# Dilated attention: another order of the tokens in each chunk of 128, and copies of the queries in block order

## The chip, the cores and the metric

The kernel runs on one core of a Trainium2 chip. The metric is the device time of one execution in microseconds (us); the median of three runs of the kernel before is 2824.8 us. Engines are named as the profile names them: PE (TensorE matmuls), PEld (its weight loads), DVE (VectorE), ACT (ScalarE), POOL (GpSimd), SP (SyncE, whose queue issues nearly all DMAs).

## The reference, cut to what matters

One layer over 2048 tokens of width 1024: a normalised input `h`, a large product with `w_in`, two branches and a merge. Branch a mixes the tokens of each chunk of 128 by a masked 128x128 matrix. Branch b, which the change is about, is attention with 16 heads of 64, in three patterns that differ in the stride of the keys:

```
DILATED_PATTERNS = ((128, 1), (512, 4), (2048, 16))   # (window, dilation)
def dilated_pattern(q, k, v, slopes, window, dilation):
    L = S // dilation                     # tokens t, t+dilation, ... form one sequence
    # blocks of 128 of such a sequence; each attends to itself and the block before
    s = einsum('bhrnqd,bhrnkd->bhrnqk', qb, kw) * Dh ** -0.5
    s = where(valid, s - slope * dist * dilation, -1e30)
    m = max(s);  p = exp(s - m);  l = sum(p);  o = p @ vw / l
    # back to token order
# the outputs of the three patterns are merged by l * exp(m - max m)
```

Numbers are kept to about float32 accuracy: float16 pairs (high and low part) for q, k, v and p, pairs of a reduced float32 for the large products.

## The kernel before, in words

Four parts follow each other. First the input is normalised and most columns of the product with `w_in` are made; q, k and v go to DRAM (`q_d`, `k_d`: one [128, 2048] float16 tensor a head with the high part in rows 0 to 63 and the low part below; `v_d`: one [2048, 130] a head). Then comes the attention window, then the last two products.

In the window `window` walks through 192 groups: 16 heads, in each head the patterns 2, 1, 0 (dilation 16, 4, 1), in each pattern four groups of four query blocks. A group has three stages, each a step or more after the other: `stage_s` (scores: two matmuls a block, Q against KH and KL, lines 407 and 408; DVE adds the bias and finds the row maxima, line 414; DVE writes the maxima into the output tile, line 417; ACT makes exp, line 422), `stage_t` (transposes of exp, lines 439 to 443) and `stage_o` (products with V, lines 456 to 458, and their copy by ACT, line 459). Blocks of pattern 2 have no block before, so their score matmuls have 128 columns; in pattern 1 one of four blocks is so, in pattern 0 one of sixteen; the others have 256. Between the stages stand matmuls of `fill`, the remaining products with `w_in` and `w_proj_a` (line 116), 416 us of them by the code's own count.

`cols` picks the columns of a block. Queries and keys stand in token order in SBUF, so a block of pattern 1 reads every fourth column of float16 (8 bytes apart), one of pattern 2 every sixteenth (32 bytes apart).

Loads and stores: `load_qk` loads Q, K (four DMAs) and the bias B of the next head when a head's pattern 1 begins. `load_v` loads V one pattern ahead, one DMA for each pattern: in pattern 2 each partition takes 16 neighbouring tokens (4160 bytes in a run), in pattern 1 four (1040 bytes), in pattern 0 one at a time (260 bytes). The outputs of patterns 2 and 1 (tile `ob`, two buffers) go to DRAM, `o_d`, with one DMA each, and come back in token order into OC, which has one buffer; pattern 0 writes into OC itself. `combine` then merges the three on DVE, ACT and POOL and, for a pair of heads, transposes and multiplies with the gate (`sbg`) and stores `yb`.

POOL splits the weights of `fill` into high and low parts (lines 85 and 86; `wraw` and the two parts have two buffers each), scales B and adds in `combine`. Every DMA of the window is issued by SP, in one order. PE's order is fixed by the code (`seg`). On the other engines and SP's queue a scheduler sets the order when the program is built, from its own estimates of when things are ready.

Of the kernel before, what the change touches and what calls it, by code (L numbers as in the profile page):

```python
# [16 lines left out]
P = 128  # L17
# [10 lines left out]
class Prog:  # L28
# [5 lines left out]

    # ---------------------------------------------------------------- setup
    def setup(self):
# [36 lines left out]

    # -------------------------------------------------------------- helpers
    def rsqrt_mean(self, out, ss, n):
# [12 lines left out]
    def wblock(self, wp, w, c0, width, scale=None):  # L88
        """columns c0..c0+width of a weight, as exact high and low parts;
        scale: [P, 1] that gets a scale under which no product with h leaves float16"""  # L90
        nc = self.nc
        raw = wp.tile([P, KC, width], F32, name="wraw", tag="wraw", bufs=256 // width)
        nc.sync.dma_start(out=raw, in_=w[:, c0:c0 + width].rearrange("(k p) n -> p k n", p=P))
        hi = wp.tile([P, KC, width], F32R, name="whi", tag="whi")
        lo = wp.tile([P, KC, width], F32R, name="wlo", tag="wlo")
        self.split_w(raw, hi, lo)
        if scale is not None:
            # |h @ w| <= |h| |w column| <= (32 max|g|) (32 max|w|)
            m = self.wk.tile([P, 2], F32, name="wm", tag="wm")
            nc.vector.tensor_reduce(out=m[:, 0:1], in_=raw, axis=AX.XY, op=ALU.max, apply_absolute_value=True)  # L100
            nc.vector.tensor_copy(m[:, 1:2], self.gmax)
            r = self.wk.tile([P, 2], F32, name="wr", tag="wr")
            nc.gpsimd.partition_all_reduce(r, m, P, bass_isa.ReduceOp.max)
            nc.vector.tensor_mul(m[:, 0:1], r[:, 0:1], r[:, 1:2])
            nc.vector.tensor_scalar(out=m[:, 0:1], in0=m[:, 0:1], scalar1=1.0 / 32.0, scalar2=1e-15,
                                    op0=ALU.mult, op1=ALU.max)
            nc.vector.reciprocal(out=scale, in_=m[:, 0:1])
        return hi, lo

    def mm3(self, out, st, mv, ks=range(KC), first=True, last=True, every=0):  # L110
        """out (+)= sum_k (st_hi + st_lo)[k].T @ (mv_hi + mv_lo)[k] in three products of exact parts;
        st, mv: functions of (part, k)"""
        nc = self.nc
        todo = [(a, b, k) for k in ks for a, b in ((0, 0), (0, 1), (1, 0))]
        for n, (a, b, k) in enumerate(todo):
            self.pe = nc.tensor.matmul(out, st(a, k), mv(b, k), start=first and n == 0,  # L116
                                       stop=last and n == len(todo) - 1)
            if every and (n + 1) % every == 0 and n + 1 < len(todo):
                yield every

    def seg(self, gen):
        """the next piece of gen, its PE work queued behind that of the piece before"""
        if self.last_pe is None:
            r = next(gen, None)
        else:
            with self.tc.issue_after(self.last_pe):
                r = next(gen, None)
        if self.pe is not None:
            self.last_pe = getattr(self.pe, "ins", self.pe)
        self.pe = None  # L130
        return r
# [6 lines left out]

    # ------------------------------------------------------- normalised input
    def alloc_X(self, tt):  # L140
# [70 lines left out]

    # ---------------------------------------------------------------- q and k
    def ev_qk(self, dst, s):
# [40 lines left out]

    # --------------------------------------------------------------- branch a
    def branch_a(self, hf, X):
# [64 lines left out]

    # ------------------------------------------------------------- gates of b
    def ev_bg(self, nb, qd, ps):
# [22 lines left out]

    # -------------------------------------------------------------- attention
    def load_qk(self, at, h):
# [5 lines left out]
        for j in range(2):  # L354
# [5 lines left out]
                                op0=ALU.mult, op1=ALU.add)  # L360
        return Q, KH, KL, B

    def load_v(self, at, h, p):
        nc = self.nc
        V = at.tile([P, 16, 130], F16, name="V", tag="V", bufs=4)
        vs = self.v_d[h]
        if p == 0:
            nc.sync.dma_start(out=V, in_=vs.rearrange("(n a) d -> a n d", a=P))
        elif p == 1:
            nc.sync.dma_start(out=V.rearrange("p (n q) d -> p n (q d)", q=4),  # L370
                              in_=vs.rearrange("(n a q) d -> a n (q d)", n=4, q=4))
        else:
            nc.sync.dma_start(out=V, in_=vs.rearrange("(a n) d -> a n d", a=P))
        return V

    def cols(self, t, p, b, n):
        """n = 1: columns of block b; n = 2: of block b and the next one"""
        if p == 0:
            return t[:, P * b:P * (b + n)]
        if p == 1:  # L380
            return t.rearrange("p (a q) -> p q a", q=4)[:, b // 4, P * (b % 4):P * (b % 4 + n)]
        return t.rearrange("p (a q) -> p q a", q=16)[:, b]

    def stage_s(self, at, G):
# [4 lines left out]
        pr = h // 2  # L389
        if p == 1:  # L390
            ob = G["O"].rearrange("p (n q) d -> p q n d", q=4)[:, g]
        else:
            ob = G["O"][:, 4 * g:4 * g + 4]
        G["ob"] = ob
# [25 lines left out]
        for i in range(4):  # L420
# [3 lines left out]
            for c in range(n):  # L424
                kb = 4 * g + i - (n - 1 - c)
                pairs.append((i, c, kb if p != 1 else kb % 4 * 4 + kb // 4, c == 0, c == n - 1))
        G["pairs"] = pairs
# [20 lines left out]
    def stage_o(self, at, G):  # L448
# [137 lines left out]

    # ------------------------------------------------------------- last phase
    def final(self):
# [78 lines left out]

    # -------------------------------------------------------------------- all
    def run(self):
# [53 lines left out]
def _tables():  # L723
    i = np.arange(P)
    slopes = (2.0 ** (-8.0 * np.arange(1, NH + 1, dtype=np.float32) / NH)).astype(np.float32)
    bias = np.zeros((NH, P, 640), np.float32)
    dist = i[:, None] + P - np.arange(2 * P)[None, :]
    ok = (dist >= 0) & (dist <= P)
    for p, dil in enumerate((1, 4, 16)):
        for h in range(NH):  # L730
# [4 lines left out]
    causal = (i[None, :] >= i[:, None]).astype(np.float32)  # L735
    return bias, causal

# [31 lines left out]
```

## Time and profile before

| | before |
|---|---|
| runs | 2823.9, 2824.8, 2834.3 us |
| span of the profiled execution | 2821.4 us (3.4 us under the median of the runs) |
| attention window | from 1467.7 to 2414 us |
| PE, DVE, ACT, POOL busy | 97%, 42%, 38%, 22% of the span |
| DMA engines, share of their time | 0.35 ahead of the window, 0.63 in it, 0.52 after it |

The span runs from the first to the last instruction that the profiler recorded. A busy PE can still be slow PE, since the time of a matmul is counted whatever holds it. The granted clock is 0.98 to 0.99 in all parts.

### The profile page before, as it was taken

What the parts mean: (1) busy time and instruction counts of PE and PEld (TensorE: products, weight loads), DVE (VectorE), ACT (ScalarE), POOL (GpSimd) and SP (SyncE); (2) the same over time, 40 slices, a digit from 0 to 9 for tenths busy, and PEclk for the clock granted to TensorE, in tenths of its full rate; (3) what the DMA queues carried; (4) which work ended last, traced back from release to release, by engine and by line L of the source; (5) the groups of instructions that cost most, each with busy time, mean ns of one, the idle gap of its engine ahead of it and who ended that gap; (6) DMA issues with size and microseconds to landing.
All of it is one profiled execution on the core that took longest, in us unless ns stands there. A gap on an engine that the chain in (4) does not pass through costs nothing.

```text
span 2821.4 us, 44790 instructions
## 1 busy us (share of the span) xinstructions
PE 2724.5 (97%) x17504; PEld 2273.2 (81%) x17504; DVE 1195.5 (42%) x3186; ACT 1063.8 (38%) x2039; POOL 625.6 (22%) x398
## 2 busy tenths in 40 slices
PE   6899899999999999999999999999999999899998
PEld 4779897888887889988877777777777777678887
DVE  6232104331003111013336666677677777555443
ACT  4312212122123222221126666666666666333221
POOL 2322211223233221212231221233333333100000
PEclk9999999999999999999999999999999999999999
DMA  7633402224345333202254556656677676665442
GB/s 230 177 101 85 93 16 76 67 87 134 101 136 155 93 102 84 66 28 68 67 163 115 153 149 169 166 169 182 186 213 221 192 208 187 205 208 183 153 151 74
DMA packets 489332, 381.68 MB, mean 135 GB/s; under 512 B 152224, under 2 KB 414752, under 8 KB 489120
## 3 DMA queue, kind: packets, MB, share of 16 engines
q1 hardware_dynamic: 488688, 378.75, 46.4%
q8 instruction: 137, 2.24, 0.3%
q14 instruction: 75, 0.61, 0.1%
q10 hardware_dynamic: 432, 0.07, 0.0%
HBM read 277.42 MB, written 101.32 MB: 134 GB/s over the span
## 4 chain that ended last, share of the span: by engine, by line
PE 84%; DMA 3%; DVE 3%; ACT 2%; issue 2%; POOL 1%; SPq 0%; DVEq 0%; ACTq 0%; POOLq 0%
PE pj L116 65%; PE ss L407 5%; PE ss L408 5%; PE pt L439 4%; PE po L456 1%; PE po L458 1%; PE po L457 1%; DMA wraw<-in_w_proj_b 1%; PE pt L297 1%; DMA v_d<-vst 1%; ACT junk L281 1%; DVE X L148 1%; PE pt L509 0%; POOL wlo L86 0%; DMA xl<-ya_d 0%
## 5 line engine op out<-in xcount | busy, mean ns | idle before, releaser
L116 PE MATMUL pj<-X,whi 128*128 128x512 f32 x4608 | 1472.0, 398 | 21.4 <-ACT whi L83 8.3
L116 PEld LDWEIGHTS pj<-X,whi 128*128 128x128 f32 x4608 | 868.2, 190 | 202.6 <-ACT whi L83 10.3
L116 PE MATMUL pj<-X,wlo 128*128 128x512 f32 x2304 | 915.5, 397 | 16.1 <-POOL wlo L86 10.8
L86 POOL TENSOR_TENSOR wlo<-wraw,whi 128x1024 fp32r<-128x1024 f32 (+1 forms) x176 | 458.5, 2606 | 763.7 <-ACT whi L83 688.3
L116 PEld LDWEIGHTS pj<-X,wlo 128*128 128x128 f32 x2304 | 437.9, 190 | 109.8 <-POOL wlo L86 12.7
L116 PE MATMUL pj<-whi,X 128*128 128x256 f32 x2048 | 360.7, 279 | 6.9 <-DVE vst L238 6.7
L83 ACT CAST whi<-wraw 128x1024 fp32r<-128x1024 f32 (+1 forms) x152 | 173.2, 1140 | 505.2 <-PE pj L116 445.7
L116 PEld LDWEIGHTS pj<-whi,X 128*128 128x128 f32 x2048 | 312.9, 188 | 8.2 <-issue 7.2
L414 DVE CUSTOM_DVE_ANT_0 S<-ss,B 128x256 f32<-128x256 f32 (+1 forms) x768 | 244.6, 361 | 143.7 <-PE ss L408 142.6
L116 PE MATMUL pj<-wlo,X 128*128 128x256 f32 x1024 | 285.6, 279 | 2.7 <-POOL vst L233 2.7
L422 ACT ACTIVATE S<-S,ob,iqk 128x128 f32<-128x128 f32 (+1 forms) x512 | 231.8, 525 | 95.4 <-DVE ob L417 95.3
L407 PE MATMUL ss<-KH,Q 128*128 128x256 f16 (+1 forms) x768 | 258.5, 356 | 6.9 <-DVE m L414 6.8
L408 PE MATMUL ss<-KL,Q 128*128 128x256 f16 (+1 forms) x768 | 264.7, 358 | 0.0
L443 DVE SCALAR_TENSOR_TENSOR pl<-pt,ph 128x512 f16<-128x512 f32 x320 | 203.4, 653 | 89.8 <-ACT ph L442 88.1
L442 ACT ACTIVATE ph<-pt 128x512 f16<-128x512 f32 x320 | 167.5, 560 | 119.6 <-PE pt L439 119.5
L116 PEld LDWEIGHTS pj<-wlo,X 128*128 128x128 f32 x1024 | 192.6, 188 | 2.9 <-POOL vst L233 2.9
L85 POOL TENSOR_SCALAR whi<-wraw 128x1024 fp32r<-128x1024 f32 x64 | 69.3, 1083 | 539.0 <-PE pj L116 508.6
L116 PE MATMUL pj<-WO,X 128*128 128x512 f32 x768 | 180.1, 395 | 0.9 <-ACT X L632 0.8
L116 PEld LDWEIGHTS pj<-WO,X 128*128 128x128 f32 x768 | 144.1, 188 | 36.2 <-ACT X L632 1.2
L439 PEld LDWEIGHTS pt<-ident,S 128*128 128x128 f32 x1200 | 146.1, 144 | 28.9 <-DVE pl L443 3.6
L439 PE MATMUL pt<-ident,S 128*128 128x128 f32 x1200 | 165.6, 275 | 2.7 <-DVE pl L443 2.7
L422 ACT ACTIVATE S<-S,OC,iqk 128x256 f32<-128x256 f32 (+1 forms) x256 | 131.8, 584 | 52.5 <-DVE OC L417 52.5
(105 smaller groups left out, 2422.5 us busy)
## 6 DMA issues: line engine op xcount, KB each, us to landing
wraw<-in_w_in SPq DMA_DIRECT2D x136, 512.0 KB, 4.1
V<-v_d SPq DMA_DIRECT2D x48, 520.0 KB, 4.2
o_d<-ob SPq DMA_DIRECT2D x32, 528.0 KB, 4.3
OC<-o_d SPq DMA_DIRECT2D x32, 528.0 KB, 5.2
wraw<-in_w_in SPq DMA_DIRECT2D x16, 1024.0 KB, 5.6
wraw<-in_w_proj_a SPq DMA_DIRECT2D x32, 512.0 KB, 5.3
wraw<-in_w_proj_b SPq DMA_DIRECT2D x32, 512.0 KB, 4.5
v_d<-vst SPq DMA_DIRECT2D x128, 65.0 KB, 3.5
```

The costliest lines, as they stand in the source:

```text
L83: nc.scalar.copy(hi, raw)
L85: nc.gpsimd.tensor_scalar(out=hi, in0=raw, scalar1=1.0, scalar2=0.0, op0=ALU.mult, op1=ALU.add)
L86: self.w_lo.tensor_tensor(out=lo, in0=raw, in1=hi.bitcast(F32), op=ALU.subtract)
L116: self.pe = nc.tensor.matmul(out, st(a, k), mv(b, k), start=first and n == 0, stop=last and n == len(todo) - 1)
L148: self.x_lo.tensor_tensor(out=X[k][1], in0=src, in1=X[k][0].bitcast(F32), op=ALU.subtract)
L407: nc.tensor.matmul(ps[:, i, :n], q, self.cols(KH, p, w0, n // P), start=True, stop=False)
L408: self.pe = nc.tensor.matmul(ps[:, i, :n], q, self.cols(KL, p, w0, n // P), start=False, stop=True)
L414: nc.vector.tensor_tensor_reduce(out=S[:, j, :n], in0=ps[:, i, :n], in1=B[:, bo:bo + n], scale=1.0, scalar=-3e38, op0=ALU.add, op1=ALU.max ...
L422: nc.scalar.activation(S[:, i, :rng[i]], S[:, i, :rng[i]], AF.Exp, bias=ob[:, i, 65:66], scale=self.iqk[:, pr:pr + 1])
L439: self.pe = nc.tensor.transpose(px[:, j * P:(j + 1) * P], G["S"][:, i, c * P:(c + 1) * P], self.ident)
L442: nc.scalar.activation(ph[:, :n], px[:, :n], AF.Copy, scale=PSCALE)
L443: nc.vector.scalar_tensor_tensor(out=pl[:, :n], in0=px[:, :n], scalar=PSCALE, in1=ph[:, :n], op0=ALU.mult, op1=ALU.subtract)
```

## The change

The 128 tokens of each chunk stand in another order throughout the kernel. Position i holds token `i % 8 * 16 + i // 8 % 4 * 4 + i // 32`. Tokens of one residue modulo 4 are then 32 neighbouring columns, and those of one residue modulo 16 are 8 neighbouring columns, in each chunk. The inputs x, `w_s`, `b_s`, the causal mask and the bias tables are given in that order, and the output is put back. What else changes:

- `cols` now picks keys of pattern 1 in runs of 32 columns (64 bytes) and keys of pattern 2 in runs of 8 (16 bytes).
- POOL makes two copies of Q a head in block order, `QP[2]` and `QP[1]` (a new tile with two buffers), so that a block's queries are 128 neighbouring columns.
- V of the patterns 1 and 2 and their outputs are moved by the new function `rows` with 16 DMAs each (32 or 8 partitions, pieces of 260 or 264 bytes) where one DMA did it. V has three buffers in place of four.
- The output tile of pattern 1 is written in the order of its groups.

```diff
 def load_qk(self, at, h):
 ...
-        return Q, KH, KL, B
+        QP = {0: Q}
+        for p in (2, 1):
+            QP[p] = at.tile([P, T], F16, name="QP", tag="QP")
+            n = 16 if p == 2 else 4
+            nc.gpsimd.tensor_copy(QP[p].rearrange("p (r c a) -> p r c a", r=n, c=16),
+                                  Q.rearrange("p (c r a) -> p r c a", r=n, c=16))
+        return QP, KH, KL, B
 def load_v(self, at, h, p):
-        V = at.tile([P, 16, 130], F16, name="V", tag="V", bufs=4)
+        V = at.tile([P, 16, 130], F16, name="V", tag="V", bufs=3)
 ...
-        elif p == 1:
-            nc.sync.dma_start(out=V.rearrange("p (n q) d -> p n (q d)", q=4),
-                              in_=vs.rearrange("(n a q) d -> a n (q d)", n=4, q=4))
         else:
-            nc.sync.dma_start(out=V, in_=vs.rearrange("(a n) d -> a n d", a=P))
+            for part, row in self.rows(V, vs, p):
+                nc.sync.dma_start(out=part, in_=row)
+    def rows(self, t, d, p):
+        if p == 1:
+            tv = t.rearrange("p (q n) d -> p n q d", q=4)
+            dv = d.rearrange("(n c q a) d -> n c a q d", n=4, c=4, q=4)
+            return [(tv[32 * c:32 * c + 32, n], dv[n, c]) for n in range(4) for c in range(4)]
+        dv = d.rearrange("(c r a) d -> c a r d", c=16, r=16)
+        return [(t[8 * c:8 * c + 8], dv[c]) for c in range(16)]
 def cols(self, t, p, b, n):
         if p == 1:
-            return t.rearrange("p (a q) -> p q a", q=4)[:, b // 4, P * (b % 4):P * (b % 4 + n)]
-        return t.rearrange("p (a q) -> p q a", q=16)[:, b]
+            c = b % 4 * 4
+            return t.rearrange("p (c q a) -> p q c a", c=16, q=4)[:, b // 4, c:c + 4 * n]
+        return t.rearrange("p (c r a) -> p r c a", c=16, r=16)[:, b]
 def stage_s(self, at, G):
-        if p == 1:
-            ob = G["O"].rearrange("p (n q) d -> p q n d", q=4)[:, g]
-        else:
-            ob = G["O"][:, 4 * g:4 * g + 4]
+        ob = G["O"][:, 4 * g:4 * g + 4]
 ...
-                q = self.cols(Q, p, b, 1)
+                q = Q[p][:, P * b:P * b + P]
 def stage_o(self, at, G):
-            if p == 2:
-                nc.sync.dma_start(out=od.rearrange("(a r) d -> a r d", r=16), in_=G["O"])
-            else:
-                nc.sync.dma_start(out=od.rearrange("(n a q) d -> a n (q d)", n=4, q=4),
-                                  in_=G["O"].rearrange("p (n q) d -> p n (q d)", q=4))
+            for part, row in self.rows(G["O"], od, p):
+                nc.sync.dma_start(out=row, in_=part)
```

The scheduler puts the DMAs of SP's queue in another order. Before, on SP, between the loads of V for two patterns of head 12 (`v_d_133`; `o_d_1_184` and `o_d_0_183` are the outputs of patterns 2 and 1 of head 11, a name ahead of `<-` is what is written):

```order
L373 DMA V<-v_d_133 128x2080
L179 DMA xl<-ya_d_139 128x512 x2
L342 DMA gal<-ga_d_150 128x512
L93 DMA wraw<-in_w_proj_a 128x8x128 x2
```

Now, on SP, from the output of pattern 2 of head 11 to the next weight block:

```order
L475 DMA o_d_1_184<-ob 8x16x66 x16
L377 DMA V<-v_d_133 8x16x130 x15
L345 DMA ma_d_158<-ma 128x512
L475 DMA o_d_0_183<-ob 32x4x66 x16
L479 DMA OC<-o_d_1_184 128x16x66
L342 DMA gal<-ga_d_150 128x512
L377 DMA V<-v_d_133 32x4x130 x4
L345 DMA ma_d_158<-ma 128x512
L377 DMA V<-v_d_133 32x4x130 x12
L342 DMA gal<-ga_d_150 128x512
L479 DMA OC<-o_d_0_183 128x16x66
L345 DMA ma_d_158<-ma 128x512
L93 DMA wraw<-in_w_proj_a 128x8x128
```

All 64 new DMAs of a head stand in one stretch there, the two loads of OC behind bursts, and the next weight block behind all of them.

DVE, the first pattern-2 groups of head 1 before (`m_11417` is the maxima of the first group):

```order
L414 ISA S,m_11417<-ss,B 128x128
L414 ISA m_11417 128x1
L417 TENSOR_SCALAR ob<-m_11417,niqk 128x4
L327 SCALAR_TENSOR_TENSOR tbg<-tbg,pj 128x512
L443 SCALAR_TENSOR_TENSOR pl<-pt,ph 128x512 x2
L414 ISA S,m_11494<-ss,B 128x128
```

and now (line 414 is 426, line 417 is 429; `m_11515`, `m_11592` and `m_11680` are the first three groups):

```order
L426 ISA S,m_11680<-ss,B 128x128
L426 ISA m_11680 128x1
L429 TENSOR_SCALAR ob<-m_11515,niqk 128x4
L429 TENSOR_SCALAR ob<-m_11592,niqk 128x4
L429 TENSOR_SCALAR ob<-m_11680,niqk 128x4
L327 SCALAR_TENSOR_TENSOR tbg<-tbg,pj 128x512
L426 ISA S,m_11751<-ss,B 128x128
```

The maxima of three groups are written together there, after the scores of the third; this happens in eight places of the window.

More of the change, by code (lines that the diff above doesn't have):

```diff
@@ L425, in stage_s @@
                 kb = 4 * g + i - (n - 1 - c)
-                pairs.append((i, c, kb if p != 1 else kb % 4 * 4 + kb // 4, c == 0, c == n - 1))
+                pairs.append((i, c, kb, c == 0, c == n - 1))
         G["pairs"] = pairs
@@ L724, in _tables @@
     i = np.arange(P)
+    tok = i % 8 * 16 + i // 8 % 4 * 4 + i // 32
+    inside = (tok, i // 32 * 32 + i % 8 * 4 + i // 8 % 4, i)
     slopes = (2.0 ** (-8.0 * np.arange(1, NH + 1, dtype=np.float32) / NH)).astype(np.float32)
     bias = np.zeros((NH, P, 640), np.float32)
-    dist = i[:, None] + P - np.arange(2 * P)[None, :]
-    ok = (dist >= 0) & (dist <= P)
     for p, dil in enumerate((1, 4, 16)):
+        key = np.concatenate([inside[p], P + inside[p]])
+        dist = inside[p][:, None] + P - key[None, :]
+        ok = (dist >= 0) & (dist <= P)
         for h in range(NH):
@@ L734, in _tables @@
             bias[h, :, 256 * p:256 * p + b.shape[1]] = b
-    causal = (i[None, :] >= i[:, None]).astype(np.float32)
-    return bias, causal
+    causal = (tok[None, :] >= tok[:, None]).astype(np.float32)
+    return bias, causal, tok
 def kernel(x, g_norm, w_in, w_s, b_s, g_v, w_proj_a, w_proj_b, w_out, g_final):
     arr = lambda v: np.ascontiguousarray(np.asarray(v))
-    bias, causal = _tables()
-    x2 = arr(x)[0]
+    bias, causal, tok = _tables()
+    x2 = arr(x)[0].reshape(T // P, P, D)[:, tok].reshape(T, D)
     ins = {
@@ L747 @@
         "w_in": arr(w_in)[0],
-        "wsT": arr(w_s)[0].transpose(2, 0, 1),
+        "wsT": arr(w_s)[0].transpose(2, 0, 1)[tok][:, :, tok],
         "causal": causal,
-        "bs": np.broadcast_to(arr(b_s)[0][None], (P, 8, P)),
+        "bs": np.broadcast_to(arr(b_s)[0][:, tok][None], (P, 8, P)),
         "g_v": arr(g_v)[0].reshape(KC, P).T,
@@ L767 @@
     r = run_bass_kernel_spmd(nc, [{"in_" + k: v for k, v in ins.items()}], core_ids=[0])
-    return r.results[0]["out_y"].reshape(1, T, D)
+    y = np.empty((T // P, P, D), np.float32)
+    y[:, tok] = r.results[0]["out_y"].reshape(T // P, P, D)
+    return y.reshape(1, T, D)
```

## The prediction

> **What bounds the kernel now.** I read the head of the page first, then the three stages, then one head of the attention window by its patterns.
>
> ```profile
> span 2821.4 us, 44790 instructions
> PE 2724.5 (97%) x17504; PEld 2273.2 (81%) x17504; DVE 1195.5 (42%) x3186; ACT 1063.8 (38%) x2039; POOL 625.6 (22%) x398
> PE 84%; DMA 3%; DVE 3%; ACT 2%; issue 2%; POOL 1%; SPq 0%; DVEq 0%; ACTq 0%; POOLq 0%
> core 0: us, PE busy (x) PEld busy (x) DVE busy (x) ACT busy (x) POOL busy (x), PEclk, DMA share, GB/s
> 1467.70:2414.00 946.30, 932.18 (x8028) 739.26 (x8028) 664.68 (x2395) 608.79 (x1364) 265.04 (x191) 0.99 0.63 177
> 1812.80:1833.10 20.30, 20.30 (x179) 15.98 (x176) 9.69 (x50) 11.54 (x29) 7.04 (x5) 1.00 0.73 188
> 1833.10:1851.10 18.00, 18.00 (x148) 13.34 (x145) 16.91 (x52) 11.95 (x28) 7.73 (x6) 1.00 0.36 114
> 1851.10:1873.30 22.20, 22.20 (x216) 18.95 (x213) 13.78 (x48) 14.30 (x31) 6.88 (x4) 1.00 0.67 190
> ```
>
> TensorE is the bound: 84% of the chain that ended last is PE, and in the attention window (1467.7 to 2414.0, the only stage that the change touches) it is busy 932 of 946 us. The last three rows are head 6: its pattern 2 (dilation 16), pattern 1 (dilation 4) and pattern 0 (dilation 1) steps. One head costs 946.3 / 16 = 59.1 us; this one 60.5. So a shorter score product is worth its whole length, until another queue needs as long.
>
> **The gain: score products.** Each group makes eight score matmuls. The order-of-time view of PE shows their pace by pattern; I read the distance from one start to the next, since the durations overlap.
>
> ```profile
> 1824.07 0.42 PE L407 MATMUL ss<-KH,Q 128*128 128x128 f16 x1
> 1824.31 0.42 PE L408 MATMUL ss<-KL,Q 128*128 128x128 f16 x1
> 1824.55 0.42 PE L407 MATMUL ss<-KH,Q 128*128 128x128 f16 x1
> ...
> 1841.64 0.28 PE L407 MATMUL ss<-KH,Q 128*128 128x128 f16 x1
> 1841.73 0.30 PE L408 MATMUL ss<-KL,Q 128*128 128x128 f16 x1
> 1841.85 0.41 PE L407 MATMUL ss<-KH,Q 128*128 128x256 f16 x1
> 1842.08 0.41 PE L408 MATMUL ss<-KL,Q 128*128 128x256 f16 x1
> ...
> 1501.18 0.22 PE L407 MATMUL ss<-KH,Q 128*128 128x128 f16 x1
> 1501.24 0.22 PE L408 MATMUL ss<-KL,Q 128*128 128x128 f16 x1
> 1501.30 0.27 PE L407 MATMUL ss<-KH,Q 128*128 128x256 f16 x1
> 1501.41 0.27 PE L408 MATMUL ss<-KL,Q 128*128 128x256 f16 x1
> ```
>
> Pattern 2, keys 32 bytes apart: 0.24 us for 128 columns. Pattern 1, keys 8 bytes apart: 0.12 for 128 (1841.73 to 1841.85) and 0.23 for 256. Pattern 0, contiguous: 0.06 and 0.11. Per column that is 1.9, 0.9 and 0.43 ns. Halving falls between 32 and 8 bytes, so what is paid seems to be a piece of 16 bytes: one key in each for pattern 2 (1.9 ns), two for pattern 1 (2 x 0.9). After the change pattern 2 reads runs of 8 keys (16 bytes) and pattern 1 runs of 32 (64 bytes); at 1.9 ns a piece, eight columns need 3.4 ns at pattern 0's pace anyway. I therefore take pattern 0's pace for both. A pattern-2 group saves 8 x (0.24 - 0.055) = 1.48 us, a pattern-1 group 2 x (0.12 - 0.055) + 6 x (0.23 - 0.11) = 0.85 us; with 64 groups each, 94.7 + 54.4 = **149 us**. The other end is nothing saved, if what costs is the jump and not the piece.
>
> The Trainium skill's page "SBUF — State Buffer" (Door 1, the note on cachelines) names the same 16 bytes, and says that two hits in a line are enough for full speed. By that, pattern 1 is already at full speed and its 54 us are not there; the trace disagrees (0.23 against 0.11 us for 256 columns), so the row decides.
>
> **POOL copies.** Two copies of 128x2048 f16 a head, 32 in all. Nearest rows, by elements:
>
> ```profile
> L85 POOL TENSOR_SCALAR whi<-wraw 128x1024 fp32r<-128x1024 f32 x58 | 63.0, 1086 | 504.1 <-PE pj L116 482.1 <-DVE pl L443 16.5 <-DMA wraw<-in_w_in 3.1
> L499 POOL TENSOR_TENSOR OC<-OC 128x256 f32<-128x256 f32 x60 | 49.0, 821 | 115.7 <-DVE ob L417 32.7 <-DVE OC L497 29.5 <-ACT ph L442 23.1
> ```
>
> 1.06 ns an element gives 2.2 us a copy, 3.2 ns (a two-input operation) 6.6 us: 70 to 210 us of POOL work on an engine busy 265 of 946 us. I take 2.2, since the copy has one input like L85. L85 waited 482 us for PE, so a copy ahead of a weight split fits; the queries are loaded most of a head (some 40 us) ahead of their first use. I charge nothing; at 6.6 us, 13 us of a 50 us head, it can delay splits (3.5 us each, one or two buffers ahead), at most a few us a head.
>
> **DVE.** After the gain the pattern-1 steps of head 6 would take 18.0 - 3.4 = 14.6 us, but DVE has 16.9 us of work there (the merge of the head before falls into them). The pattern-2 steps have 20.3 - 5.9 = 14.4 for 9.7. PE can run about two groups ahead, so part of the 2.3 us is carried over; I take half, 1.2 us x 16 = **19 us** (0 to 37).
>
> **SP's queue.** Four DMAs a head (V and O, patterns 1 and 2) become 64. How many SP issues now, and for how long:
>
> ```profile
> V<-v_d SPq DMA_DIRECT2D x44, 520.0 KB, 4.2
> ...
> xl<-yb_d SPq DMA_DIRECT2D x7, 256.0 KB, 5.8
> ...
> 1073.36 1.90 SPq L242 DMA_DIRECT2D v_d<-vst  x4
> ...
> 1817.23 0.60 SPq L355 DMA_DIRECT2D KH<-k_d  x1
> 1817.87 0.60 SPq L356 DMA_DIRECT2D KL<-k_d  x1
> 1818.51 0.58 SPq L358 DMA_DIRECT2D B<-in_bias  x1
> ...
> SPq L470 <- DMA o_d<-ob: 63.0, 23, 4.7
> ```
>
> The first two are the first and last of the window's 18 issue rows; their counts add to 442, 27.6 a head. Four short-run DMAs in a row take 1.90 us, 0.48 each; DMAs on 64 partitions follow each other in 0.64. The new ones have short runs and 8 or 32 partitions, so either may be nearer. A head then issues 27.6 - 4 + 64 = 87.6, or 42 us (0.48) to 56 us (0.64), against 50 us that PE will need (59.1 less 149 / 16 = 9.3). Taking the middle, 0.56, gives 49: SP goes from a fifth of its time to about all of it, and it still has waits, such as the 2.7 us (63.0 / 23) for an output burst to land before OC is read back. The bursts also bunch: from a head's third pattern-1 group to the next head's second pattern-2 group SP has all 64, 31 to 41 us, where PE will need 7 + 21 + 7 = 35. Behind a late SP stand the weight block that POOL splits for PE, `gal` for DVE's products, and OC for the merge, which DVE executes in order. In the order, OC of pattern 1 stands behind the next head's 16 V loads, 8 to 10 us. I charge 3 us a head, **48 us** (0 to 12 us a head).
>
> The Trainium skill's page "DMA: Bandwidth & Descriptors" (Issuing engines are not separate DMA queues) calls an issue's time usually small relative to the DMA itself. By that this term would be nothing and the sum -149 + 19 + 8 = -122 us, 2703; the rows disagree, since 0.48 to 0.64 us times 16 is longer than the 4.2 us in which a whole V lands now.
>
> **DMA traffic.** The 520 KB transfers fall into 2048 pieces of 260 or 264 bytes. One such transfer alone (OC) is in the trace:
>
> ```profile
> GB/s 0 0 0 9 82 115 96 113 211 253 272 282 272 272 284 272 277 279 275 272 282 270 249 197 115 49 7 0 0 0 0 0 0 0 0 0 0 0 0 0
> q1 hardware_dynamic: 2064, 0.54, 57.9%
> ```
>
> In that 4.5 us window (1735 to 1739.5) short pieces reach 272 to 284 GB/s, and take 0.579 x 4.5 = 2.6 us of all 16 DMA engines. The window's mean is 177 GB/s at a share of 0.63, 281 at full: short pieces cost almost nothing more. Four transfers a head move at the same rate. If eight partitions can use only half of the DMA engines, those two a head take 5.2 us: on them 0.63 x 59.1 = 37 us grows to 42 in a head of 50. I charge 0.5 us a head, **8 us** (0 to 2 a head). V's third instead of fourth buffer costs nothing: a load comes one pattern ahead and at most three patterns are live.
>
> **DVE's order.** In eight places the maxima of three pattern-2 groups are written together, since their tile is awaited from an output burst; exp of the first then starts two groups later, some 2 to 4 us each. It is inside the SP charge.
>
> **Sum.** -149 + 19 + 48 + 8 = -74 us. The profiled span is 2821.4, 3.4 under the median of 2824.8 (start and end outside the span, untouched): 2824.8 - 74 = 2750.8, rounded to **2750 us**.
>
> **The rivals.** Changes under 0.5% (14 us) can't be told from none.
> (1) Nearly all of the gain arrives: issues take 0.48 us, bursts hide behind SP's idle time (now four fifths), DVE's surplus is carried over. Loss 15 us: 2690. For it: each load is a pattern ahead. Against: 42 us of issue beside waits in a 50 us head, in one ordered queue.
> (2) Slower: SP is the bound. With 0.64 us an issue (the 64-partition rows) the issues are 56 us; two OC waits of 2.7 make 61.5, and 0.5 us more of waits for data 62. That is 2.9 a head over 59.1: 2824.8 + 46 = 2871. It decides from (59.1 - 5.9) / 87.6 = 0.61 us an issue. For it: the back-to-back rows at 0.64; against: 0.48 for short runs.
> (3) No change: an issue near 0.6, or runs of 16 bytes that cost like jumps, so that 54 us of pattern 1 meet a charge of about the same: 2811 to 2839.
> (4) The copies don't do what they should: runs read at the old pace in both patterns and all charges stay: 2824.8 + 75 = 2900.
>
> **How the numbers follow.** My forecast, a gain about half eaten (2710 to 2811): 0.45. Rival 1 (2680 to 2710): 0.19. Rival 3: 0.14. Rival 2: 0.19. Rival 4: 0.03. Faster 0.64, no change 0.14, slower 0.22. The likeliest case's own range is 2710 to 2800. The range, 2690 to 2870, leaves out about half of rival 1, half of rival 2 and rival 4.
>
> **What would show it.** Right: score matmuls of patterns 1 and 2 start 0.11 us (256) and 0.055 (128) apart; the window shrinks from 946 to about 872 us; SP's bursts run at 0.48 to 0.64 us; PE's idle time grows, before products that wait for weights, `gal` or exp. POOL copies take 2.2 us. Wrong: if bursts pace at 0.65 or more and heads last 60 us, rival 2; if score matmuls keep 0.2 us, the step on 16-byte pieces failed; if PE stays at 98% of the window, the SP and DVE charges were too high.

## The result and the profile after

The changed kernel takes 3215.7 us (3211.8 to 3220.8) beside 2824.4 us for the kernel before on the same chip: ratio 1.138, 95% interval 1.136 to 1.141. It is slower by 391 us where 2750 was forecast, and above the range (2690 to 2870). The head of the page after, and then the attention window (1472.3 to 2782.0) and in it head 6 by its patterns 2, 1 and 0 (columns as in the prediction):

```profile
span 3210.1 us, 46024 instructions
PE 2677.6 (83%) x17504; PEld 2258.8 (70%) x17504; DVE 1256.7 (39%) x3186; ACT 1068.7 (33%) x2039; POOL 692.8 (22%) x430
PE 62%; DVE 9%; DMA 7%; SPq 6%; ACT 6%; issue 3%; POOL 2%; DVEq 0%; POOLq 0%; ACTq 0%
```

```profile
1472.30:2782.00 1309.70, 879.26 (x8030) 719.83 (x8030) 721.61 (x2392) 611.76 (x1361) 329.86 (x221) 0.83 0.53 128
1887.90:1925.50 37.60, 17.85 (x177) 14.79 (x174) 10.26 (x45) 10.50 (x26) 10.06 (x7) 0.68 0.72 167
1925.50:1945.40 19.90, 16.68 (x149) 13.67 (x146) 19.65 (x50) 12.39 (x28) 12.21 (x9) 0.91 0.51 133
1945.40:1971.70 26.30, 23.02 (x217) 19.12 (x214) 13.80 (x53) 15.89 (x34) 6.83 (x4) 1.00 0.29 64
```

The window grew from 946 to 1310 us, and that is nearly the whole loss. PE is busy for less time than before (879 against 932 us) and idle for 430 us, where it was idle for 14. No other engine is full: DVE 722, ACT 612, POOL 330 of 1310 us, and the DMA engines fell from a share of 0.63 to 0.53. The score products did become faster, as forecast (PE in order of time, a pattern-1 group):

```profile
1925.54 0.22 PE L419 MATMUL ss<-KH,QP 128*128 128x128 f16 x1
1925.60 0.22 PE L420 MATMUL ss<-KL,QP 128*128 128x128 f16 x1
1925.65 0.27 PE L419 MATMUL ss<-KH,QP 128*128 128x256 f16 x1
1925.76 0.27 PE L420 MATMUL ss<-KL,QP 128*128 128x256 f16 x1
```

They start 0.06 and 0.11 us apart. What PE waits for is in the view of waits, cut to PE and the window (total us, times, longest). First the longest rows of before, then those of after:

```profile
PE ss L407 <- DVE m L414: 6.8, 6, 2.4
PE po L456 <- ACT ob L459: 3.1, 3, 1.1
```

```profile
PE pj L116 <- POOL whi L85: 292.9, 15, 33.6
PE pt L451 <- DVE pl L455: 45.0, 26, 6.4
PE pj L116 <- POOL wlo L86: 20.8, 15, 2.5
```

Fifteen waits for a split weight, up to 33.6 us long, make 293 us. One of them, from PE, POOL and SP in order of time (start, length, what; idle time before it in brackets):

```profile
2020.79 1.22 PE L116 MATMUL pj<-X,whi 128*128 128x512 f32 x2 [25.61 <-POOL whi L85]
```

```profile
2019.69 1.05 POOL L85 TENSOR_SCALAR whi<-wraw 128x1024 fp32r<-128x1024 f32 x1 [0.78 <-DMA wraw<-in_w_in]
```

```profile
1982.54 2.71 SPq L520 DMA_DIRECT2D sbg<-bg_d  x2
1985.35 1.32 SPq L377 DMA_DIRECT2D V<-v_d  x3
1993.73 0.94 SPq L523 DMA_DIRECT2D yb_d<-yb  x2
1994.72 6.17 SPq L377 DMA_DIRECT2D V<-v_d  x13
2001.00 0.36 SPq L336 DMA_DIRECT2D gb_d<-tga  x1
...
2003.96 3.14 SPq L353 DMA_DIRECT2D Q<-q_d  x1
...
2009.56 0.58 SPq L358 DMA_DIRECT2D B<-in_bias  x1
2010.24 2.23 SPq L93 DMA_DIRECT2D wraw<-in_w_in  x2
```

PE stands still from 1995.2. The weight that it needs is issued at 2010.24, and POOL splits it from 2019.69. Until then SP stood for 7 us ahead of a store (of `yb`, 1986.7 to 1993.7), then issued the other 13 pieces of V in 6.2 us, two stores, and the next head's Q, K and B, all of which stand ahead of the weight in its one order. POOL's own order is late too: ahead of this split stand the merge's additions, for which POOL sat idle for 47.4 us until DVE had OC, then a query copy and the scaling of B, all done at 2018.9. An earlier weight alone would have let this split start only 0.8 us sooner; OC, Q and B come through SP's queue as well. Over the window POOL waits 450 us, in 16 places, for a weight itself. Before the change PE never waited for a weight in the window.

### The profile page after: what moved, and what is told of

It is laid out like the page before. It is cut to its first block, busy times and chain, and to the rows that moved or that the text cites. A ratio compares the mean times of both kernels' runs of the same rounds, so it can differ in the third digit from the quotient of the medians.

```text
span 3210.1 us, 46024 instructions
## 1 busy us (share of the span) xinstructions
PE 2677.6 (83%) x17504; PEld 2258.8 (70%) x17504; DVE 1256.7 (39%) x3186; ACT 1068.7 (33%) x2039; POOL 692.8 (22%) x430
## 4 chain that ended last, share of the span: by engine, by line
PE 62%; DVE 9%; DMA 7%; SPq 6%; ACT 6%; issue 3%; POOL 2%; DVEq 0%; POOLq 0%; ACTq 0%
PE pj L116 53%; ACT S L434 3%; PE pt L451 2%; SPq L377 2%; DVE S L426 2%; SPq L475 2%; DVE pl L455 2%; POOL wlo L86 1%; DVE OC L506 1%; DMA wraw<-in_w_in 1%; PE ss L419 1%; PE ss L420 1%; DMA wraw<-in_w_proj_a 1%; PE pt L297 1%; ACT ph L454 1%
## 5 line engine op out<-in xcount | busy, mean ns | idle before, releaser
L116 PE MATMUL pj<-X,whi 128*128 128x512 f32 x4608 | 1505.5, 406 | 319.8 <-POOL whi L85 292.9
L116 PEld LDWEIGHTS pj<-X,whi 128*128 128x128 f32 x4608 | 887.5, 195 | 507.8 <-POOL whi L85 297.9
L116 PE MATMUL pj<-X,wlo 128*128 128x512 f32 x2304 | 932.5, 405 | 41.4 <-POOL wlo L86 31.6
L116 PEld LDWEIGHTS pj<-X,wlo 128*128 128x128 f32 x2304 | 447.6, 194 | 145.9 <-POOL wlo L86 44.3
L426 DVE CUSTOM_DVE_ANT_0 S<-ss,B 128x256 f32<-128x256 f32 (+1 forms) x768 | 237.5, 360 | 177.6 <-PE ss L420 176.9
L451 PE MATMUL pt<-ident,S 128*128 128x128 f32 x1200 | 182.8, 285 | 71.0 <-DVE pl L455 45.0
L468 PE MATMUL po<-V,ph 128*128 128x65 f16 x1200 | 138.7, 198 | 11.7 <-ACT ob L471 11.0
L470 PE MATMUL po<-V,pl 128*128 128x65 f16 x1200 | 135.9, 198 | 9.3 <-DVE pl L455 9.3
```

The lines of the kernel that those rows point to most:

```text
L426: nc.vector.tensor_tensor_reduce(out=S[:, j, :n], in0=ps[:, i, :n], in1=B[:, bo:bo + n], scale=1.0, scalar=-3e38, op0=ALU.add, op1=ALU.max ...
L451: self.pe = nc.tensor.transpose(px[:, j * P:(j + 1) * P], G["S"][:, i, c * P:(c + 1) * P], self.ident)
L468: nc.tensor.matmul(o, ph[:, sl], V[:, kb, 64:129], start=first, stop=False)
L470: self.pe = nc.tensor.matmul(o, pl[:, sl], V[:, kb, 64:129], start=False, stop=last)
```

## The experiments

Each kernel was run beside the kernel before, whose median was 2824 to 2830 us in all of these runs; the ratio's 95% interval is in brackets. At first three causes stood against each other: the number of DMAs that SP issues, the short pieces in which data now move, and POOL's copies with what they do to DVE.

**Is it the pieces, the short runs, or the copies?** Four kernels take these apart.

The changed kernel with one DMA in place of each 16 (short pieces kept; V's rows and the outputs' then stand at other places than the computation needs):

```diff
-            for part, row in self.rows(V, vs, p):
-                nc.sync.dma_start(out=part, in_=row)
+            nc.sync.dma_start(out=V, in_=vs.rearrange("(n a) d -> a n d", a=P))
```

> The changed kernel, but V and the outputs of patterns 1 and 2 are moved by one DMA each, in the same 260 and 264 byte pieces (the rows land in other places, so the numbers of the output are not the reference's). It takes away the number of DMAs and leaves the short runs of keys, the POOL copies, the three V buffers and the size of the pieces. Theory A (the loss is in SP's queue: 64 DMAs a head, behind which the weight blocks of PE stand): the gain of 149 us arrives less some 20 to 40 on DVE, 2690 to 2720 us. Rival B (POOL's copies and their waits delay the weight splits): it stays over 3100. Rival C (the short pieces load the DMA engines): over 3000.

Measured: 2769.6 us, 0.980 [0.977, 0.983]. The same with the long runs of the kernel before:

> The changed kernel with V and the outputs of patterns 1 and 2 moved by one DMA each, in the long pieces of the kernel before (4160, 1040, 4224, 1056 bytes; the rows land in other places than the reference's). Against the run with one DMA in short pieces (2770 us) it changes the size of the pieces alone. Theory S (the 93 us that are missing there from the gain of 149 went to the DMA engines, whose share was 0.86 of the window there against 0.63): 2690 to 2735 us. Theory D (they went to DVE, ACT and POOL, which have more work than PE in parts of a head): 2755 to 2780, no difference to short pieces.

Measured: 2770.0 us, 0.980 [0.978, 0.982]. Pieces of 260 bytes cost no time beside long runs (the DMA engines' share of the window rises from 0.67 to 0.86), and without the 60 extra DMAs a head the change gains 2%. The other way round, the kernel before with V and O of the dilated patterns cut into 16 DMAs each, and nothing else:

```diff
-            nc.sync.dma_start(out=V, in_=vs.rearrange("(a n) d -> a n d", a=P))
+            dv = vs.rearrange("(a n) d -> a n d", a=P)
+            for c in range(16):
+                nc.sync.dma_start(out=V[8 * c:8 * c + 8], in_=dv[8 * c:8 * c + 8])
```

> The kernel before, with V and the outputs of patterns 1 and 2 cut into 16 DMAs each, of 8 or 32 partitions, in the long pieces of before. Nothing else of the change. The scheduler here leaves weight loads between the bursts, one about every 20 DMAs, where the changed kernel has them behind all 64. Theory A1 (it is the place of the weight loads in SP's order that costs): 2830 to 2900 us, PE hardly waits for weights. Theory A2 (it is the number of DMAs, wherever they stand; an issue is 0.47 us, so 28 us more of SP a head): 2950 to 3200. Rivals B and C: 2825 to 2840, no change.

Measured: 3185.5 us, 1.127 [1.124, 1.130]. The number of DMAs alone loses 355 us, and PE waits for the same thing (waits of PE in its window):

```profile
PE pj L116 <- POOL whi L85: 225.2, 29, 16.5
PE pj L116 <- POOL wlo L86: 41.4, 29, 3.7
```

The changed kernel without POOL's copies (`QP[p] = Q`, so other queries are multiplied):

> The changed kernel without POOL's copies: the score matmuls of all patterns take their 128 queries as neighbouring columns of Q itself (other queries than the reference's, the same shapes). The bursts stay. Theory A: 3150 to 3216 us, the copies (2.2 us, 32 of them) were beside other work. Rival B (the copies and their waits in POOL's order delay the weights): 2700 to 2900.

Measured: 3186.7 us, 1.127 [1.124, 1.130]: in this kernel the copies cost 29 us, not 390.

**How does the loss grow with the number?** The kernel before with 4 and with 8 DMAs in place of one (12 and 28 more a head):

> The kernel before with V and the outputs of patterns 1 and 2 cut into 4 DMAs each of 32 partitions: 16 where before has 4 and the run with 16 each has 64 a head (that one lost 355 us, 0.37 us for each of the 60 more). Theory L (each DMA adds its issue time to the time of a head, since SP always issues or waits): 12 x 0.37 x 16 = 71 us more, 2890 to 2905. Theory T (SP has room, and the loss begins when it is full): 2825 to 2845.

> The same with 8 DMAs each of 16 partitions, 32 a head. Theory L: 28 x 0.37 x 16 = 166 us more, 2980 to 3000. Theory T: 2835 to 2900.

Measured: 2933.8 us, 1.038 [1.035, 1.041], and 3125.6 us, 1.105 [1.103, 1.108]. With 12, 28 and 60 more a head the loss is 107, 299 and 355 us: 0.56, 0.67 and 0.37 us for each DMA. It is no straight line, and no threshold either, since the first twelve are paid in full.

**Is it the place of the weight loads?** In the order that the scheduler wrote, I counted for each of the window's 64 products how many weight loads of later products stand on SP ahead of its last store. The mean is 2.84 before and 1.62 after; with 4, 8 and 16 pieces in the kernel before it is 1.55, 1.00 and 1.00. So the weights are also queued later. First, the changed kernel with the window's weights loaded through POOL's queue:

```diff
-        nc.sync.dma_start(out=raw, ...)
+        q = nc.gpsimd if self.w_hi is nc.gpsimd else nc.sync
+        q.dma_start(out=raw, ...)
```

> The changed kernel, but the 64 weight blocks of the window (wraw) are loaded by DMAs that POOL issues, so they stand in no queue with the bursts; all 64 bursts of V and outputs stay on SP. Theory A1 (weight loads behind the bursts): the wait of POOL for wraw (291 + 159 us) nearly goes, 2750 to 2900 us. Theory A2 (SP is too late for everything: gal, OC, V as well): 3050 to 3200. Rival B (POOL is the trouble): slower than 3216, since POOL gets more to do.

Measured: 3115.1 us, 1.103 [1.099, 1.106]: 101 us come back, and most of the loss stays. Then the changed kernel with its weights on SP, but loaded two products earlier in the program (`load(n + 3)` behind the split of product n), and the kernel before with its weights held back:

```diff
+            with self.tc.issue_after(last_store_of_an_earlier_product):
+                nc.sync.dma_start(out=raw, in_=src)
```

> The changed kernel with all its 64 pieces a head on SP, but with the load of a window weight written two products earlier in the program (behind the split that frees its buffer), so that it stands earlier in SP's order. Read from the order that the scheduler wrote: at the row of a product's last store, 2.84 loads of later weights stand ahead of it on SP in the kernel before, 1.62 after the change (none in 12 of 64 products), 2.30 here (never under 2). Theory L (the pieces made the scheduler put the weight loads late in the queue, and PE waits for load and split): most of what was lost comes back, 2770 to 2880 us. Theory Q (what costs is the time that SP spends on 60 more issues a head, 0.45 us each, whatever their order): little changes, 3120 to 3220 us.

> The kernel before, with no DMA added; each weight load of the window is queued on SP behind the last store of the product before, so that on average 0.05 loads stand ahead instead of 2.84. Theory L: each of 64 products shows PE a load (4.4 us) and a split (3.4 us), together about 8 us, of which attention's own work covers a part: slower by 250 to 500 us, 3070 to 3330. Theory Q: SP issues no DMA more than before, so at most a few us a head: 2825 to 2870 us.

> The kernel before, with no DMA added; each weight load of the window is queued behind the last store of the product but one, 1.03 loads ahead on average instead of 2.84. The kernels before with 8 and with 16 pieces have a mean of 1.0 and lost 299 and 355 us. Theory L in its pure form (the place in the order alone decides): 3000 to 3180 us. Theory Q: 2825 to 2860 us. If both are needed (a late place costs little while SP comes to it soon, and much once 60 issues stand around it): 2830 to 2950 us, while the one with nothing ahead is far slower.

Measured: early weights 3131.0 us, 1.108 [1.106, 1.111]; the kernel before with no load ahead 3448.3 us, 1.220 [1.218, 1.222]; with one ahead 2868.2 us, 1.014 [1.013, 1.016]. A load that stands behind the store of the product just ahead is ruinous without any added DMA, but one product of lead costs 40 us only, where the same lead with 28 or 60 more DMAs costs 299 or 355. And with early weights PE's wait for them is gone while most of the loss stays (PE's waits in the window of the kernel with early weights):

```profile
PE pj L133 <- DVE ma L362: 110.7, 16, 24.9
PE pt L469 <- DVE pl L473: 54.8, 32, 5.9
PE ss L437 <- DVE m L444: 46.6, 18, 8.2
...
PE pj L133 <- POOL whi L85: 19.0, 4, 7.7
```

Now `ma` comes last, DVE's product with the gate `gal`, which SP loads too: the wait moved to the next thing in the queue. DVE's own waits for `gal` make 41 of these 111 us; what the rest is was not followed. The theory of the weights' place is a part (85 us), not the whole.

**Is it the sharing of one queue?** The projections' loads were given to POOL and their stores to ACT (`self.lq()` and `self.sq_()` in place of `nc.sync` at lines 93, 179, 328, 336, 342, 345, 520 and 523).

> The changed kernel with SP left to attention's own DMAs (queries, keys, bias, V, O in their 64 pieces a head): in the window the weight, gate and activation loads of the projections are issued by POOL, their stores by ACT. Theory Q (one queue in program order: the pieces hold up everything that stands behind them, weights first and, when those are early, the gate loads and stores): with the projections off SP the time falls to 2770 to 2840 us. Theory P (the pieces hold up attention itself: V and O arrive late because 32 pieces stand ahead of them, and PE has nothing else to do): 3000 to 3110 us, as with weights alone on POOL (3115).

Measured: 3225.9 us, 1.140 [1.139, 1.142]. This told nothing about the two theories, since a new tie came in (SP's waits in the window, first rows):

```profile
SPq L481 <- DMA ma_d<-ma: 144.1, 19, 15.5
SPq L481 <- DMA yb_d<-yb: 90.8, 18, 10.3
SPq L481 <- DMA gb_d<-tga: 85.8, 9, 20.2
```

SP's output pieces wait for stores that ACT issued and that have nothing to do with them; all rows of this kind make 592 us. The program shows why:

```
L481 DMA o_d_0_169<-ob 32x4x66 [waits DMAHW7_49,DVE_49,Activation_49]
L481 DMA o_d_0_169<-ob 32x4x66 [waits DMAHW0_49]
L481 DMA o_d_0_169<-ob 32x4x66 [waits DMAHW1_49]
```

All DMAs of SP and ACT take eight completion semaphores in turn, and each waits for the last user of its own. A burst of 16 goes round twice, so it waits for whatever else is in the ring.

**Does an issue cost by itself?** The kernel before, its V and O moved as before, with 60 loads a head that nothing reads, 15 behind each V load and O store of the dilated patterns. (The expectation says 32 KB each; 8 partitions x 16 runs x 16 bytes are 2 KB.)

```diff
+        for c in range(15):
+            self.nc.sync.dma_start(out=du[8 * c:8 * c + 8], in_=src[8 * c:8 * c + 8, :, 0:4])
```

> The kernel before, its V and O moved as before, with 60 loads a head more that nothing reads (32 KB in 8 partitions x 16 runs each, 15 behind each V load and each O store of the dilated patterns): SP's issues as in the kernel before with 16 pieces, without any data that waits for them. Theory Q (every issue that SP is given in this window is paid nearly in full, whatever it moves, since SP's other time is waiting for data that comes out of the loads behind it): of 60 x 16 issues at about 0.4 us, 380 us, three quarters or more: 3080 to 3220 us. Theory P (the pieces cost because V and O arrive late): 2825 to 2900 us. By the order, 0.89 loads of later weights stand ahead of a product's last store, against 2.84 in the kernel before.

> The same idle loads, with the weight loads written two products earlier (2.31 ahead on average). What of the loss is the late weights, and what all the rest of SP's queue. If the weights are nearly all of it: 2830 to 2920 us. If the queue as a whole is the bound, as the changed kernel with early weights says (3131 against 3216, a quarter of the loss back): 2980 to 3120 us.

Measured: 3241.2 us, 1.145 [1.143, 1.147], and with early weights 3154.2 us, 1.115 [1.113, 1.117]. The idle loads lose 411 us, and early weights give 87 of them back, as they gave 85 to the changed kernel. PE's longest wait is the known one, and the issues of the idle loads (min, median, max ns) are dearer than the 0.4 us that I expected:

```profile
PE pj L116 <- POOL whi L85: 256.0, 34, 17.6
```

```profile
L367 SPq DMA_DIRECT2D du<-in_bias x960: 661/673/1384, 1451.1 to 2825.2; - x192
```

So time on SP's queue is what is lost, with no data in it that anyone waits for. SP's time in each window, summed over the trace's records of its issues:

| kernel | more DMAs a head | window | issuing | the rest: waits |
|---|---|---|---|---|
| before | 0 | 946 | 232 | 715 |
| before, 4 pieces | 12 | 1050 | 337 | 713 |
| before, 8 pieces | 28 | 1239 | 460 | 779 |
| before, 16 pieces | 60 | 1279 | 609 | 669 |
| changed | 60 | 1310 | 652 | 658 |
| changed, early weights | 60 | 1223 | 656 | 567 |
| idle loads | 60 | 1348 | 894 | 454 |
| idle loads, early weights | 60 | 1259 | 911 | 348 |

SP's rest in the kernel before looks like room for 715 us, but most of it isn't. By the written order a store waits for a result, which comes from a weight that was loaded behind the store before it; 424 us of SP's waits there end with a result of DVE or ACT, but how many are tied in this way was not measured. 12 more DMAs use none of that rest, 60 pieces 46 to 57 us, and even idle loads with early weights only half of it. The window grows by 0.5 to 1.3 of the issue time that is added; for the changed kernel, beside itself with one DMA each in long runs (889 us, 241 of them issuing), it is 1.0.

**A version that beats both.** An order by the residue modulo 4 alone keeps V in token order, so the dilated patterns need one DMA again (V of pattern 0 takes four), and POOL copies the queries for all three patterns; `cols` of pattern 2 reads `[:, b % 4, b // 4]` of `"p (c q a r) -> p q r c a"`, keys 8 bytes apart.

> A version meant to keep part of the gain with few DMAs. Tokens of a chunk stand by residue modulo 4 alone (position i holds token 4 (i % 32) + i // 32); keys of pattern 1 are read in runs of 64 bytes, of pattern 2 at 8 bytes, of pattern 0 contiguously. V is stored in token order (8 stores where 4 were), so V and outputs of patterns 1 and 2 move by one DMA each as before; V of pattern 0 takes four. POOL copies the queries of all three patterns (six copies a head); DVE multiplies by the gate through a permuted view. Score matmuls save 8 x (0.24 - 0.12) us a group in pattern 2 and 0.85 in pattern 1, together 61 + 54 = 115 us. Theory S: 2720 to 2750 us. Theory D: 2750 to 2790. If the number of DMAs has no part in the loss of the changed kernel: over 3000.

Measured: 2816.6 us, 0.996 [0.995, 0.998], above the ranges of theories S and D. The score groups are some 121 us shorter in all (medians of 0.87 us in pattern 2 and 0.77 in pattern 1), but the window shrinks by 34 us only, from 946 to 912, and begins 22 us later. With more of the projections' products beside the merge of a head (`yield 0.6` for `0.0` in `combine`, the sum in `window` raised to match), and with that and the copies on ACT (`nc.scalar.copy`):

> The kernel with order by residue mod 4 (2817 us) and 3 us a head more of projection products interleaved with the combining of a head, fewer elsewhere. Per phase it had PE busy 16.0 of 19.0 us with DVE busy 17.6 (one phase), and PE busy 20.1 of 20.7 (another). Theory D (in the one phase DVE sets the pace and PE has room; in the other PE does): products moved from the second to the first gain 1.5 to 3 us a head, 2770 to 2795 us. Rival (DVE's chain is only stretched by the extra products): 2810 to 2840 us.

> The same with the three copies of queries on ACT instead of POOL, which is left idle for DVE's sake: DVE's operations beside POOL's copies took 415 ns instead of 305 and 835 instead of 546, some 60 us in all. Theory D: DVE's 40 to 60 us come back and a half of it shows in the time: 2745 to 2780 us. Rival (ACT's copies of 2 us stand in the way of the exponentials): 2810 to 2900 us.

Measured: 2806.7 us, 0.992 [0.991, 0.994], faster than both kernels; with copies on ACT 2830.4 us, 1.000 [0.999, 1.001]. The first gained 10 us of the 22 to 47 expected. With the copies on ACT DVE is busy for 671 instead of 696 us of the window, as expected, but ACT for 718 instead of 609, and PE's longest wait is now for `pl` (38 us, where it was 9), the low part that DVE makes from ACT's `ph`. That this is why the copies lose 24 us there was not tested.

## Why the prediction was wrong

The step that failed is SP's queue: "I charge 3 us a head, **48 us** (0 to 12 us a head)". Measured: the changed kernel less the same without pieces, 3215.7 - 2770.0 = 446 us, 27.9 a head, more than twice the upper bound. The issue price was not too low: all issues of the window took 0.48 us in the mean (652 us for 1360), the low end of the forecast, and V's pieces 263/380/1402 ns:

```profile
L377 SPq DMA_DIRECT2D V<-v_d x480: 263/380/1402, 1494.7 to 2726.0; - x160
```

What was wrong was to add up the issues (42 to 56 us), set them against PE's 50 us a head, and count only "such as the 2.7 us" of the waits. SP's waits before were 715 us, 45 a head, and most of them stay when issues are added (658 us): a head takes 41 us of issues and 41 of waits, 82 in all. What would stand behind a late SP was named rightly: the weight block, `gal` and OC. Rival 2 had the right culprit and the wrong rule, that it "decides from (59.1 - 5.9) / 87.6 = 0.61 us an issue": it decided at 0.48, because the question was never whether the issues fit into a head. The range failed with it. A warning was at hand in SP's waits of before, of which I read one line (`OC`, 63 us) and not the sum; that these waits are no room the kernel with idle loads showed.

The other terms of the sum:

- The score products gained what was forecast, in both patterns. Groups of eight matmuls fell from 1.92 to 0.45 us (pattern 2) and from 1.62 to 0.77 (pattern 1), medians; with 64 groups each that is 94 + 54 = 148 us, where 149 was forecast. The reading of a piece of 16 bytes holds for all that was run.
- DVE was charged 19 us (0 to 37). Without pieces, 2770 us is 55 under the 2824.8, so 94 of the 149 us forecast are lost, with the copies and everything else. In the window of that kernel (889 us) PE is idle for 70 us, where it was idle for 14; 50 us of its waits are for DVE and 16 for ACT, so this term was too small as well. The other part, PE busy for 819 us where 932 less 149 is 783, is not explained. In head 6 of the kernel with one DMA each (long runs) the pattern-2 steps fall to 15.1 us and the pattern-1 steps do not gain at all, as DVE is busy for 18.44 of 18.70 us:

```profile
1780.30:1795.40 15.10, 14.85 (x179) 12.87 (x176) 9.79 (x44) 10.65 (x27) 7.56 (x6) 1.00 1.02 230
1795.40:1814.10 18.70, 15.48 (x148) 12.44 (x145) 18.44 (x51) 12.37 (x28) 9.64 (x8) 1.00 0.38 120
1814.10:1836.60 22.50, 22.36 (x216) 18.96 (x213) 15.38 (x55) 14.84 (x32) 6.90 (x4) 1.00 0.64 199
```

- POOL's copies took 1.9 us, as forecast (2.2), and were charged nothing; removing them won 29 us. They slow DVE, which is busy for 722 us of the window with them and 680 without, for the same operations; that this is where the 29 us went is likely, but not shown:

```profile
L365 POOL COPY QP<-Q x32: 1885/1892/2622, 1449.1 to 2671.0; 128x2048 f16<-128x2048 f16 x32
```

- DMA traffic was charged 8 us. Short pieces cost no time (2769.6 with them, 2770.0 with long runs), but the reading that they cost the DMA engines "almost nothing more" was wrong: at the same rate of 188 to 189 GB/s their share is 0.86 with short pieces and 0.67 with long runs. The reason of the charge, transfers on eight partitions, was not tested, since both kernels move V over 128; nor were DVE's order in the eight places and V's third buffer.

## What to carry to other kernels

A queue that issues loads and stores in one order is not free while it waits: before adding DMAs to it, ask what stands behind each of its waits. That its issues and waits fill a stage does not tell whether there is room, since what is not issuing counts as waits here, and the two make up the window in every row of the table. What told it here were DMAs that move nothing of use, added to the kernel before. The window grew by 0.5 to 1.3 of the issue time that was added, however small the transfers (2 KB), and with the DMA engines busy for only 0.50 to 0.57 of the windows with 60 more DMAs a head. Look for a layout in which a tensor still moves in one DMA, even if its products then run slower, and read off a faster engine's next bound (here DVE, in one phase) before counting the gain.

## What the hardware showed that I had not expected

Matmuls became slower when PE had to wait. The windows of the kernel before with 16 pieces and with weights held back, beside 932 us at 0.99 before (after the window stand its length and PE busy; the granted clock is the third number from the end; the second window holds 196 matmuls more than the first):

```profile
1473.00:2751.00 1278.00, 1009.20 (x8025) 780.05 (x8025) 682.77 (x2389) 613.66 (x1359) 263.59 (x191) 0.86 0.51 130
1473.00:3030.00 1557.00, 1128.01 (x8221) 850.14 (x8222) 701.16 (x2427) 630.33 (x1381) 278.35 (x198) 0.80 0.39 109
```

So a wait of PE costs more than its length: 77 of the 332 us by which the first window grew are PE's own work at a lower clock. The traces' records of the granted clock bear this out. They hold 1 and one half alone, in stretches that are multiples of 3.41 us. In the first of these two windows PE is busy for 168 us at one half, and in the kernel before for 13 us; half of the difference, 78 us, is what the lower clock costs. The stall shown above, of the changed kernel, in three stretches (PE idle, PE at work again, PE later):

```profile
1997.40:2020.70 23.30, 0.00 (x0) 0.00 (x0) 10.31 (x19) 2.69 (x6) 8.21 (x7) 0.50 0.96 229
2020.70:2028.00 7.30, 6.00 (x28) 4.06 (x29) 0.49 (x3) 0.38 (x1) 5.76 (x4) 0.50 0.30 89
2028.10:2060.00 31.90, 31.90 (x313) 27.14 (x312) 22.44 (x86) 25.59 (x55) 8.73 (x5) 1.00 0.35 85
```

The clock fell at 1997.3, 2.1 us after PE had stopped, and came back at 2028.1, 7.3 us after PE had started again. The Trainium skill's page "TensorE: Matmul & The Clock Gate" (What's actually happening) says that the clock is halved after an idle window of about 3.4 us; the stretches in the record agree.

POOL holds up DVE's small operations until its own operation ends. The same two additions on 128x16 elements, before and in the kernel with copies and one DMA each in long runs (min, median, max ns):

```profile
L484 DVE TENSOR_TENSOR mn<-lw x15: 167/171/574, 1538.5 to 2376.0; 128x16 f32<-128x16 f32 x15
L485 DVE TENSOR_TENSOR mn<-mn,lw x15: 162/172/177, 1538.7 to 2376.3; 128x16 f32<-128x16 f32 x15
```

```profile
L499 DVE TENSOR_TENSOR mn<-lw x15: 164/569/2180, 1529.7 to 2318.2; 128x16 f32<-128x16 f32 x15
L500 DVE TENSOR_TENSOR mn<-mn,lw x15: 161/175/2344, 1530.4 to 2320.5; 128x16 f32<-128x16 f32 x15
```

In that kernel 20 of the 96 operations that write `mn` take over 0.5 us. Each of them lies beside an operation of POOL and ends within 0.05 us of that one's end: nine beside the low part of a weight (`wlo`, 2.4 us), five beside the scaling of B, three beside the high part of a weight and only three beside a copy of queries. The longest, with the POOL operation beside it (start, length, what):

```profile
2306.69 2.38 POOL L86 TENSOR_TENSOR wlo<-wraw,whi 128x1024 fp32r<-128x1024 f32 x1
2306.75 2.36 DVE L494 TENSOR_TENSOR mn<-mn,OC 128x16 f32<-128x16 f32 x1
```

The Trainium skill's page "SBUF — State Buffer" (SBUF: two separate sides) says that a DVE operation with two inputs in SBUF and a POOL operation that reads SBUF exclude each other for the whole instruction; these rows agree, 2.3 us at most on L500 against a median of 0.18.

What stays open: why the price of one more DMA falls from 0.67 us (28 a head) to 0.37 (60 a head); a part of it is that an added issue itself falls from 0.51 to 0.39 us by the table. Open is also how the loss divides between the place of the loads in the written order and the waits in that order. The runs show a fifth of it to be the weights' place (85 of 446, 87 of 411 us); the rest was not divided. The turn of the eight semaphores is not the main part where SP issues everything: SP's waits that end when a DMA lands make 37 us of the changed kernel's window and 72 us before, while those that end with a result of DVE or ACT make 486 and 424.
